# A hybrid decoder layer on one core: one copy moves to ScalarE, and large matrix products move between the stages of a recurrence

## The chip, the core and the metric

The kernel runs on one core of a Trainium2 chip. The core has five engines that work side by side: TensorE multiplies matrices (PE in the profile, with its weight loads as PEld), VectorE works on whole tiles (DVE), ScalarE copies and evaluates functions (ACT), GpSimd does some small work (POOL), and SyncE issues most of the transfers (SP). Each has its own list of instructions and goes through it in order; an instruction waits where its operands are not there yet. The metric is the device time of one execution in microseconds (us). Lower is better.

## The reference

The layer works on x, 512 positions of 2048 channels, in float32. Cut to what matters:

```python
h = rms_norm(x, norm_g)
z = h @ w_in          # r, k, v (1024 columns each), decay and rate inputs (64 each), gate (1024), pool input and pool gate (1024 each)
zs = zs + (token_shift(zs) - zs) * mu                      # r, k, v, decay and rate inputs
decay = exp(-exp(-softplus(-(w0 + tanh(wd) @ w_up)) - 0.5)); a = sigmoid(a0 + ad @ a_up)
kk = k * k_k;  kk = kk / max(norm of kk in each head, 1e-12);  k = k * (1 + (a - 1) * k_a)
# 16 heads of 64 channels; for each position t, with a state S of 64 x 64 in each head:
S = S (diag(w_t) - kk_t^T (a_t * kk_t)) + v_t^T k_t;   y_t = S r_t
y_rwkv = (head_group_norm(y) * ln_w + ln_b + bonus) * silu(gate)
d = trailing-window means of the pool input over 2, 4, 8, 16 positions, minus the input
y_pool = (d @ w_pool, per group of 256 channels) * pool_scale * silu(pool gate)
x = x + concat(y_rwkv, y_pool) @ w_out
x = x + sigmoid(x @ w_pg + b_pg) * (p @ w_ple)
out = rms_norm(x, final_g)
```

## The kernel before

*Large products.* Each large product is one matmul of 128 x 128 weights with 128 x 512 data. Float32 accuracy is reached by splitting both sides in two parts of a shorter format, `hi` and `lo` (`wsplit`, L132 and L133, for weights; `split`, L137 and L138, for data), and by three products per block (`mm3`, L156). The products of `h @ w_in` are made in blocks of 128 columns: `zk`, `zr`, `zv`, `zg` for the eight *pairs* of heads 0 to 7, and `zb` for sixteen *pool units*. A pool unit of the first kind ends in a chain of running sums on VectorE (L397 to L401, tiles `u` and `sw`); one of the second kind multiplies with `w_pool` (`pp`). All these products are one stream, `big`, 2,352 matmuls after the first normalisation. `pump(n)` issues the next n of them at the place where it stands in the code (in threes; `debt` carries what was too much). `need` issues as many as it takes until a given block is done. So the places and sizes of the pumps set what TensorE does while it would wait for the small work between them. The order on TensorE (PE) is the order of the code (`keep_in_program_order`). On VectorE and ScalarE the order is set by a scheduler that works with estimated times, so that an edit can change it at places far from the edit.

*The recurrence.* The 512 positions are cut into 8 chunks of 64, and within a chunk the recurrence is solved with an inverse of a triangular matrix. For each pair j these steps run:

- `prepare(j)` makes the operands `ar` and `bk` on VectorE (its last step is L541, the second half of `bk`), `scores(j)` multiplies them on TensorE (`pbo`, then `pm`) and sends the result through memory to the layout of the inversion, and `invert(j)` solves 32 x 32 triangles by 62 small VectorE steps (L593, L597).
- `gather(j)` completes the inverse. On TensorE: `pv` and `pbk` (transposes of v and `bk`, copied by ScalarE to `uv` and `bkn`), `pump(H4)`, `pmv` (the right-hand sides of all chunks in one psum tile, copied by ScalarE to `mv`, L648), `pss` (the norms of the *next* pair's keys; `norm_key`: ScalarE takes the root, L504, and VectorE the maximum, L505), `pump(H5)`, `pyt` (the transposes of the previous pair's result, `finish`: `yo` on ScalarE and VectorE, and its store to `yd`, L799), `pump(HX)`, then `pq` (from `y1`, a VectorE transpose at L669 that may only be issued behind L505) and `px`, each with `pump(H1)` behind it.
- `recur(j)` goes through the chunks. A chunk has three *hops*, each a small matmul whose result an engine copies for the next one: `py` (TensorE) to `zs` (VectorE, L721), `pu` to `uv` (ScalarE, L731), `ps` to the new state `sbd` (VectorE, L740 in the first chunk and L742 in the others; two tiles, `sbd0` and `sbd1`, take turns). A pump stands behind each hop: HC = (7, 7, 8) products. In the first chunk there is no state yet, so `zs` is a plain copy of `mv` (L725), and in place of the third pump `between` issues `pump(H3)`, the scores of the next pair and `pump(H2)`. Three steps of the next pair's inversion are made at each hop from the tenth on. After each fourth chunk, ScalarE copies `py` to `ysb` (L763), and after the last the group norm runs on VectorE (L772 to L787).

The sizes are H1 = 6, H2 = 16, H3 = 20, H4 = 6, H5 = 10, HX = 24.

*The end of the recurrence.* After pair 7, `pump(H2)` and `finish` of pair 7 are issued, then whatever is left in the stream (`pump(10 ** 6)`). ScalarE's queue loads `pn` (the embeddings p, L840) and the tiles `yin` (L858), which read back the sixteen stored blocks of `yd`. Both lie in memory that the recurrence's pool `rw` gives back when it closes, and wait until its last tile has been read, which is the store of pair 7's `yo`. TensorE transposes `pn` (`ppt`, split into `phi` and `plo`), and the products with `w_out` (`acc_o`) begin as soon as the first `yin` is split into `yhi` and `ylo`. Then come the products with `w_pg` (`acc_g`), the small `pple`, and the last normalisation.

Of the kernel before, what the change touches and what calls it, by code (L numbers as in the profile page):

```python
# [34 lines left out]
def trunk_kernel(ctx: ExitStack, tc: tile.TileContext, x, p, norm_g, w_in, mu, w0, w_up, a0, a_up,  # L35
                 k_k, k_a, r_k, ln_w, ln_b, w_pool, pool_scale, w_out, w_ple, w_pg, b_pg, final_g, out):
    nc = tc.nc
    PSUM = bass.MemoryType.PSUM
    x, p, w_in, w_out, w_ple, w_pg = x[0], p[0, 0], w_in[0], w_out[0], w_ple[0], w_pg[0]
# [303 lines left out]
    zsp = [rw.tile([P, P], F32, name=f"zs{i}") for i in range(2)]  # L343
# [93 lines left out]
    def pump(n):  # L437
        debt[0] += n
        while debt[0] > 0:
            c = next(big, None)  # L440
            if c is None:
                debt[0] = 0
                return
            debt[0] -= c
# [6 lines left out]

    pws, kks, late = {}, {}, [None]

    H1, H2, H3, H4, H5 = 6, 16, 20, 6, 10

    def decay_and_rate(j):

# [156 lines left out]
    def gather(j):  # L614
        d = st_[j]
        bk, v_, mt = d.pop("bk"), d.pop("v_"), d["mt"]
        if j + 1 < NJ:
            prepare_key(j + 1)
            decay_and_rate(j + 1)

        uv = rw.tile([P, NCH, P], F32, name=f"uv{j}", tag="uv")
        ps = psM.tile([P, T], F32, name=f"pv{j}", tag="m")
        for tt in range(NT):
            tr(ps[:, tt * P:(tt + 1) * P], v_[:, tt * P:(tt + 1) * P], ident)
        pv = ps.rearrange("p (t c) -> p t c", c=P)
        nc.scalar.copy(uv[0:64, 0::2, :], pv[0:64])
        nc.scalar.copy(uv[64:128, 1::2, :], pv[64:128])


        bkn = rw.tile([P, NCH, P], F32, name=f"bkn{j}", tag="bkn")  # L630
        for hf in range(2):
            ps = psM.tile([P, T], F32, name=f"pbk{j}_{hf}", tag="m")
            for i in range(4):
                ch = 4 * hf + i
                tr(ps[:, i * P:(i + 1) * P], bk[:, ch // 2, 2 * (ch % 2):2 * (ch % 2) + 2, :], ident)
            nc.scalar.copy(bkn[:, 4 * hf:4 * hf + 4, :], ps.rearrange("p (c n) -> p c n", n=P))

        pump(H4)

        ps = psM.tile([P, 8, C], F32, name=f"pmv{j}", tag="m")  # L640
        for u in range(8):
            for par in range(2):
                pb, kb = 64 * (1 - par), 64 * par
                h = u % 2
                mm(ps[pb:pb + 64, u, :], mt[kb:kb + 64, par, u, 1 - par, :],
                   uv[kb:kb + 64, 2 * (u // 2) + par, 64 * h:64 * h + 64], start=True, stop=True)
        mv = rw.tile([P, 4, P], F32, name=f"mv{j}", tag="mv")
        nc.scalar.copy(mv.rearrange("p q (h t) -> p (q h) t", h=2), ps)  # L648

        d.update(uv=uv, bkn=bkn, mv=mv)  # L650
        if j + 1 < NJ:
            norm_key(j + 1)
        pump(H5)
        if pending:
            pending.pop()()
        pump(HX)

        x1 = d["x1"]

        def units(fn):  # L660
            for u in range(8):
                for par in range(2):
                    fn(u, par, 64 * (1 - par))

        y1 = rw.tile([P, 8, 32], F32, name=f"y1{j}", tag="tm")

        with tc.issue_after(late[0].ins):
            for pb in (0, 64):
                yt = nc.vector.transpose(y1[pb:pb + 32], x1[pb:pb + 32, :, 0:32])  # L669
        if j + 1 < NJ:  # L670
            with tc.issue_after(yt.ins):
                scale_key(j + 1)
        ps3 = psM.tile([P, 8, 32], F32, name=f"pq2{j}", tag="m")
        units(lambda u, par, pb: mm(ps3[pb + 32:pb + 64, u, :],
                                                  mt[pb:pb + 32, par, u, 1 - par, 32:64],
                                                  y1[pb:pb + 32, u, :], start=True, stop=True,
                                                  tile_position=(pb, pb + 32)))
        q2t = rw.tile([P, 8, 32], F32, name=f"q2{j}", tag="xw")
        for pb in (0, 64):
            nc.scalar.copy(q2t[pb + 32:pb + 64], ps3[pb + 32:pb + 64])  # L680
        pump(H1)
        ps4 = psM.tile([P, 8, 32], F32, name=f"px2{j}", tag="m")
        units(lambda u, par, pb: mm(ps4[pb:pb + 32, u, :], q2t[pb + 32:pb + 64, u, :],
                                                  x1[pb + 32:pb + 64, u, 32:64], start=True, stop=True,
                                                  tile_position=(pb + 32, pb)))
        for pb in (0, 64):
            nc.scalar.copy(x1[pb:pb + 32, :, 32:64], ps4[pb:pb + 32])
        pump(H1)


    def recur(j, work, between):
        d = st_.pop(j)
        pw, ar, mt, bv, uv, bkn, mv, x1 = (d[n_] for n_ in ("pw", "ar", "mt", "bv", "uv", "bkn", "mv", "x1"))
# [15 lines left out]
        for ch in range(NCH):  # L709
            par, q = ch % 2, ch // 2  # L710
            pb = 64 * (1 - par)
            cur, nxt = sbd[ch % 2], sbd[(ch + 1) % 2]
            pcc = pw[:, ch, C:C + 1]
            sl = slice((ch % 4) * P, (ch % 4 + 1) * P)
            if ch % 4 == 0:
                py = psY.tile([P, T], F32, name=f"py{j}_{ch}", tag="y")
            zs = zsp[par]
            if ch > 0:
                mm(py[:, sl], ar[:, q, 2 * par:2 * par + 2, :], cur, start=ch in (1, 4), stop=True,
                                 skip_group_check=True)  # L720
                lead[0] = nc.vector.tensor_tensor(zs[pb:pb + 64], py[pb:pb + 64, sl], mv[pb:pb + 64, q, :], ALU.add)  # L721
                step()
                pump(HC1)
            else:
                nc.vector.tensor_copy(zs[pb:pb + 64], mv[pb:pb + 64, q, :])  # L725

            psu = psS.tile([P, T], F32, name=f"pu{j}_{ch}", tag="s")
            mm(psu[:, 0:P], x1[:, 2 * q:2 * q + 2, :], zs, start=True, stop=True)
            for h in range(2):
                hc = slice(64 * h, 64 * h + 64)  # L730
                nc.scalar.copy(uv[pb:pb + 64, ch, hc], psu[hc, hc])  # L731
            step()
            pump(HC2)
            if ch < NCH - 1:
                pss = psS.tile([P, T], F32, name=f"ps{j}_{ch}", tag="s")
                mm(pss[:, 0:P], bkn[:, ch, :], uv[:, ch, :], start=True, stop=True)
                for h in range(2):
                    hc = slice(64 * h, 64 * h + 64)
                    if ch == 0:
                        lead[0] = nc.vector.tensor_scalar(nxt[hc, hc], pss[hc, hc], pcc[hc], None, ALU.mult)  # L740
                    else:
                        lead[0] = nc.vector.scalar_tensor_tensor(nxt[hc, hc], pss[hc, hc], pcc[hc], s0p[hc, :],  # L742
                                                                 ALU.mult, ALU.add)
                s0p = rw.tile([P, C], F32, name=f"s0p{j}_{ch}", tag="s0p", bufs=2)
                pcn = pw[:, ch + 1, C:C + 1]
                if ch < NCH - 2:
                    for h in range(2):
                        hc = slice(64 * h, 64 * h + 64)
                        nc.gpsimd.tensor_scalar(s0p[hc, :], nxt[hc, hc], pcn[hc], None, ALU.mult)  # L749
            if ch % 4 == 3:  # L750
                for qq in range(2):
                    for h in range(2):
                        for pr in range(2):
                            c_ = ch - 3 + 2 * qq + pr
                            yr = slice(64 * pr, 64 * pr + 64)
                            o_ = (2 * qq + pr) * P + 64 * h
                            mm(py[yr, o_:o_ + 64], mt[:, pr, 2 * (c_ // 2) + h, pr, :],
                                             uv[:, c_, 64 * h:64 * h + 64], start=False, stop=True,
                                             skip_group_check=True)
                py4 = py.rearrange("p (s c) -> p s c", c=P)  # L760
                for pr in range(2):
                    yr = slice(64 * pr, 64 * pr + 64)
                    nc.scalar.copy(ysb[yr, q - 1:q + 1, :], py4[yr, pr::2, :])  # L763
            step()
            if ch == 0:
                between()
            else:
                pump(HC3)
# [31 lines left out]

        pending.append(finish)

    HC, HT, HX = (7, 7, 8), 130, 24
    HS, HN = 9, 3
    pending = []
    need("k", 0)
# [9 lines left out]
    for _ in invert(0):  # L816
        pass
    pump(HT)
    gather(0)
    for j in range(NJ):  # L820
        def between():
# [7 lines left out]
        recur(j, invert(j + 1) if j + 1 < NJ else iter(()), between)  # L829
        if j + 1 < NJ:  # L830
            gather(j + 1)
    pump(H2)
    pending.pop()()
    s2a.close()
    psB = ctx.enter_context(tc.tile_pool(name="psB", bufs=3, space=PSUM))
# [229 lines left out]
```

## Time and profile before

| | |
|---|---|
| median of 3 runs | 1123.04 us (1122.91 to 1123.46) |
| the profiled execution | 1124.35 us, its span 1122.6 us |
| mean granted TensorE clock | 0.993 of full speed |
| matmuls | 6,090 records, busy 96% of the span |
| VectorE, ScalarE, GpSimd | busy 63%, 41%, 7% |

How the rows that follow are read. The page's first part gives the busy time of each engine, its share of the span and its number of instructions. A row of a timeline has the start of an instruction in us, its duration, engine, line, operation and tiles, and in square brackets how long the engine had been idle and what ended that. A row of the chain of waits has the start and length of a step on the path that ended last. A row of TensorE's waits names the waiting tile, what released it, and then the sum in us, the number of waits and the longest. A row of a table by windows has the stretch, its length, then busy time and number of instructions of PE, PEld, DVE, ACT and POOL, the granted clock (1.00 is full speed), the busy share of the DMA engines and the rate in GB/s. A group's row gives its busy time and the mean duration in ns behind the bar. A matmul's recorded duration is longer than the distance to the next one, since they are pipelined.

### The profile page before, as it was taken

The page shows a single profiled execution, that of the slowest core. Times are in us where ns is not written, and L with a number is a line of the kernel's source. Part 1 is how long each engine was busy: PE and PEld are TensorE (multiplying, and loading weights), DVE is VectorE, ACT ScalarE, POOL GpSimd, SP SyncE. Part 2 cuts the span into 40 slices and gives each one's busy share as a digit, 9 for nine tenths or more (in the row PEclk, how much of TensorE's full clock was granted, in tenths as well). Part 3 has the DMA queues.
Part 4 walks back from the last instruction along what each step waited for, and adds up shares of the span by engine and source line. Part 5 has one row for each costly group of instructions (what it writes and reads, how often), then busy time and mean ns, then how long its engine had stood idle before and what let it go on. Part 6 is the DMA issues. An engine that isn't in the chain of part 4 may idle for free. (4 is left out here: it accounts for less than half of the span.)

```text
span 1122.6 us, 17272 instructions
## 1 busy us (share of the span) xinstructions
PE 1081.4 (96%) x6090; PEld 880.6 (78%) x6090; DVE 709.3 (63%) x1861; ACT 459.9 (41%) x920; POOL 75.2 (7%) x184
## 2 busy tenths in 40 slices
PE   5999999999999998999999999999999999999995
PEld 4888887877877876878778787778888888888885
DVE  6677868778588687687885955564243332525446
ACT  7643536336336353363362343252222232424333
POOL 2100010110110100101101102000000000000001
PEclk9999999999999998999999999999999999999998
DMA  7433332423423332324234233465343444434244
GB/s 228 122 92 96 101 105 69 114 85 82 121 78 93 99 77 71 100 74 110 79 89 120 74 104 96 150 215 174 115 161 125 138 145 155 150 104 151 94 132 150
DMA packets 173877, 130.17 MB, mean 116 GB/s; under 512 B 34165, under 2 KB 139230, under 8 KB 173790
## 3 DMA queue, kind: packets, MB, share of 16 engines
q1 hardware_dynamic: 157694, 103.89, 31.6%
q10 hardware_dynamic: 16096, 25.17, 6.9%
q8 instruction: 48, 0.79, 0.3%
q14 instruction: 39, 0.32, 0.1%
HBM read 113.82 MB, written 14.68 MB: 114 GB/s over the span
## 5 line engine op out<-in xcount | busy, mean ns | idle before, releaser
L133 DVE TENSOR_TENSOR wlo_g<-raw_g,whi_g 128x512 fp32r<-128x512 f32 x88 | 59.4, 684 | 78.6 <-ACT whi_g L132 78.4
L156 PE MATMUL zb<-hhi,whi_b 128*128 128x512 f32 x256 | 107.2, 419 | 0.0
L133 DVE TENSOR_TENSOR wlo_o<-raw_o,whi_o 128x512 fp32r<-128x512 f32 x64 | 43.8, 691 | 93.7 <-ACT whi_o L132 93.7
L156 PE MATMUL acc_o<-wlo_o,yhi 128*128 128x512 f32 x256 | 99.9, 390 | 0.6 <-DVE wlo_o L133 0.6
L156 PE MATMUL zb<-hhi,wlo_b 128*128 128x512 f32 x256 | 100.5, 392 | 0.0
L156 PE MATMUL acc_o<-whi_o,ylo 128*128 128x512 f32 x256 | 100.3, 392 | 0.0
L132 ACT CAST whi_g<-raw_g 128x512 fp32r<-128x512 f32 x88 | 54.3, 623 | 112.2 <-PE acc_g L156 62.1
L156 PE MATMUL zb<-hlo,whi_b 128*128 128x512 f32 x256 | 100.0, 391 | 0.0
L156 PE MATMUL acc_o<-whi_o,yhi 128*128 128x512 f32 x256 | 99.4, 391 | 0.5 <-ACT yhi L137 0.5
L156 PE MATMUL acc_g<-whi_g,x2hi 128*128 128x512 f32 x224 | 86.5, 386 | 0.0
L156 PE MATMUL acc_g<-wlo_g,x2hi 128*128 128x512 f32 x224 | 86.4, 386 | 0.0
L156 PE MATMUL acc_g<-whi_g,x2lo 128*128 128x512 f32 x224 | 86.3, 385 | 0.0
L132 ACT CAST whi_o<-raw_o 128x512 fp32r<-128x512 f32 x64 | 39.7, 623 | 101.1 <-PE acc_o L156 93.6
L749 POOL TENSOR_SCALAR s0p<-sbd,pw 64x64 f32<-64x64 f32 x96 | 52.9, 551 | 331.9 <-DVE sbd L742 255.3
L132 ACT CAST whi_b<-raw_b 128x512 fp32r<-128x512 f32 x64 | 39.6, 619 | 73.5 <-PE zv L156 27.7
L133 DVE TENSOR_TENSOR wlo_b<-raw_b,whi_b 128x512 fp32r<-128x512 f32 x64 | 43.8, 685 | 29.0 <-ACT whi_b L132 28.5
L156 PEld LDWEIGHTS acc_o<-wlo_o,yhi 128*128 128x128 f32 x256 | 48.1, 188 | 11.4 <-DVE wlo_o L133 1.5
L156 PEld LDWEIGHTS zb<-hhi,wlo_b 128*128 128x128 f32 x256 | 48.0, 188 | 10.9
L156 PEld LDWEIGHTS acc_o<-whi_o,yhi 128*128 128x128 f32 x256 | 48.1, 188 | 10.5 <-ACT yhi L137 0.7
L156 PEld LDWEIGHTS acc_o<-whi_o,ylo 128*128 128x128 f32 x256 | 48.1, 188 | 10.0 <-DVE ylo L138 0.4
L597 DVE TENSOR_TENSOR xw<-xw,tm 128x60 f32<-128x60 f32 (+24 forms) x248 | 51.9, 209 | 6.3
L156 PEld LDWEIGHTS zb<-hhi,whi_b 128*128 128x128 f32 x256 | 48.3, 189 | 8.7
(290 smaller groups left out, 2568.2 us busy)
## 6 DMA issues: line engine op xcount, KB each, us to landing
raw_b<-in_w_in_dram SPq DMA_DIRECT2D x64, 256.0 KB
raw_o<-in_w_out_dram SPq DMA_DIRECT2D x64, 256.0 KB
raw_g<-in_w_pg_dram SPq DMA_DIRECT2D x64, 256.0 KB
raw_k<-in_w_in_dram SPq DMA_DIRECT2D x32, 256.0 KB
raw_r<-in_w_in_dram SPq DMA_DIRECT2D x32, 256.0 KB
raw_v<-in_w_in_dram SPq DMA_DIRECT2D x32, 256.0 KB
raw_g<-in_w_in_dram SPq DMA_DIRECT2D x32, 256.0 KB
n<-nd SPq DMA_DIRECT2D x16, 256.0 KB
```

Source lines behind the costliest of these rows:

```text
L132: nc.scalar.copy(hi, raw)
L133: nc.vector.tensor_tensor(lo, raw, hi.bitcast(F32), ALU.subtract)
L156: i = nc.tensor.matmul(*a, **k)
L597: nc.vector.tensor_tensor(xw[:, 0:n_, s + 1:32], xw[:, 0:n_, s + 1:32], tm[:, 0:n_, 0:w_], ALU.add)
L749: nc.gpsimd.tensor_scalar(s0p[hc, :], nxt[hc, hc], pcn[hc], None, ALU.mult)
```

## The change

Three things are edited. The copy of the first chunk's right-hand side to `zs` no longer stands in `recur` as a VectorE copy from `mv` (L725 before); ScalarE makes it in `gather`, straight from the psum tile of `pmv`, ahead of the `mv` copy. Large products are placed otherwise: H3 from 20 to 16, H4 from 6 to 8, HC from (7, 7, 8) to (8, 8, 8), HX from 24 to 16. And the pump ahead of pair 7's `finish` takes 32 products (HE) instead of 16 (H2). The stream itself is the same.

```diff
-    H1, H2, H3, H4, H5 = 6, 16, 20, 6, 10
+    H1, H2, H3, H4, H5, HE = 6, 16, 16, 8, 10, 32
...
         mv = rw.tile([P, 4, P], F32, name=f"mv{j}", tag="mv")
+        nc.scalar.copy(zsp[0][64:128, :].rearrange("p (h t) -> p h t", h=2), ps[64:128, 0:2, :])
         nc.scalar.copy(mv.rearrange("p q (h t) -> p (q h) t", h=2), ps)
...
                 step()
                 pump(HC1)
-            else:
-                nc.vector.tensor_copy(zs[pb:pb + 64], mv[pb:pb + 64, q, :])
...
-    HC, HT, HX = (7, 7, 8), 130, 24
+    HC, HT, HX = (8, 8, 8), 130, 16
...
         if j + 1 < NJ:
             gather(j + 1)
-    pump(H2)
+    pump(HE)
     pending.pop()()
```

In the changed kernel the new copy is L648, lines 649 to 723 stand one further down, and lines from 724 on one further up.

VectorE of the kernel before, at the beginning of pair 4's recurrence: the end of `prepare(5)` (L540, L541), a pool unit's running sums (`sw4`, `u4`) and the copy to `zs0`.

```order
L397 TENSOR_TENSOR sw4_1_5273<-u4_5271 128x511
L398 COPY sw4_1_5273<-u4_5271 128x1
L540 TENSOR_TENSOR kk5_5098<-kk5_5098,tha5_5125 128x512
L397 TENSOR_TENSOR sw4_2_5276<-sw4_1_5273 128x510
L398 COPY sw4_2_5276<-sw4_1_5273 128x2
L541 TENSOR_TENSOR bk5_5301<-kk5_5098,ipw5_5118 128x4x128
L400 TENSOR_TENSOR sw4_2_5276<-sw4_2_5276,rc1_504 128x4
L725 COPY zs0_566<-mv4_5171 64x128
L401 SCALAR_TENSOR_TENSOR u4_5271<-sw4_2_5276,u4_5271 128x512
```

The copy stands behind L541 and most of the running sums. In the changed kernel it stands on ScalarE, in pair 4's gather:

```order
L636 COPY bkn4_5150<-pbk4_1_5157 128x512
L462 CAST uaz0_568<-ur6_5302 64x128
L461 CAST as6_5309<-ar6_5306 128x128
L462 CAST uaz1_569<-ar6_5306 64x128
L648 COPY zs0_566<-pmv4_5172 64x128
L649 COPY mv4_5189<-pmv4_5172 128x512
L504 ACT_TABLE_LOAD
L504 ACTIVATE kk5_5113<-pss5_5192 128x512
```

It is now directly ahead of `mv`, and the root of the next pair's norms (L504) comes behind both.

VectorE in pair 5's gather, from the maximum of pair 6's norms (L505) to their reciprocal (L509), before:

```order
L505 TENSOR_SCALAR kk6_5803<-kk6_5803 128x512
L669 STREAM_TRANSPOSE y15_5939<-x15_5706 32x256
L133 TENSOR_TENSOR wlo_g6_1_3263<-raw_g6_1_3260,whi_g6_1_3262 128x512
L797 TENSOR_TENSOR yo4_5897<-yo4_5897,bv4_4613 128x512
L669 STREAM_TRANSPOSE y15_5939<-x15_5706 32x256
L798 TENSOR_TENSOR yo4_5897<-yo4_5897,sg4_4703 128x512
L133 TENSOR_TENSOR wlo_g6_2_3269<-raw_g6_2_3266,whi_g6_2_3268 128x512
L509 RECIPROCAL kk6_5803<-kk6_5803 128x512
```

and in the changed kernel:

```order
L505 TENSOR_SCALAR kk6_5824<-kk6_5824 128x512
L133 TENSOR_TENSOR wlo_g6_3_3291<-raw_g6_3_3288,whi_g6_3_3290 128x512
L397 TENSOR_TENSOR sw5_1_5916<-u5_5914 128x511
L398 COPY sw5_1_5916<-u5_5914 128x1
L796 TENSOR_TENSOR yo4_5935<-yo4_5935,bv4_4628 128x512
L397 TENSOR_TENSOR sw5_2_5919<-sw5_1_5916 128x510
L398 COPY sw5_2_5919<-sw5_1_5916 128x2
L797 TENSOR_TENSOR yo4_5935<-yo4_5935,sg4_4699 128x512
L133 TENSOR_TENSOR wlo_k7_0_3297<-raw_k7_0_3294,whi_k7_0_3296 128x512
L400 TENSOR_TENSOR sw5_2_5919<-sw5_2_5919,rc1_504 128x4
L670 STREAM_TRANSPOSE y15_5955<-x15_5724 32x256
L401 SCALAR_TENSOR_TENSOR u5_5914<-sw5_2_5919,u5_5914 128x512
```

Between L505 and the two transposes of `y1` stand a pool unit's sums, two weight parts and both steps of `yo`, where one weight part and one step of `yo` stood.

TensorE around the transposes of pair 7's result (`pyt7`), the last step of the recurrence, before:

```order
L156 MATMUL zb15_7774<-hhi_134,wlo_b15_0_4676 128x512
L160 MATMUL pyt7_7784<-ident_94,ysb7_7374 128x128 x4
L156 MATMUL zb15_7774<-hhi_134,whi_b15_0_4675 128x512
L156 MATMUL zb15_7774<-hlo_135,whi_b15_0_4675 128x512
L156 MATMUL zb15_7774<-hhi_134,wlo_b15_0_4676 128x512
L156 MATMUL zb15_7774<-hhi_134,whi_b15_1_4681 128x512
```

and after:

```order
L156 MATMUL pp15_7826<-dl3_7518,whi_wp15_0_4740 128x512
L156 MATMUL pp15_7826<-dh3_7517,wlo_wp15_0_4741 128x512
L160 MATMUL pyt7_7835<-ident_94,ysb7_7399 128x128 x4
L848 MATMUL ppt0_7860<-ident_94,pn0_7854 128x128 x2
L848 MATMUL ppt1_7867<-ident_94,pn0_7854 128x128
L848 MATMUL ppt0_7860<-ident_94,pn1_7856 128x128 x2
L848 MATMUL ppt1_7867<-ident_94,pn0_7854 128x128
L848 MATMUL ppt1_7867<-ident_94,pn1_7856 128x128 x2
L156 MATMUL acc_o0_0_7946<-whi_o0_8_7952,yhi_7877 128x512
```

`pyt7` had 24 large products between pair 7's last `py` and itself, and 45 behind it before `ppt`; now 33 stand ahead of it and none behind it.

## Prediction

> **What bounds the kernel now.** I read the page's busy shares first, then TensorE's waits, then the timelines at the longest waits, and last the chain that ended last.
>
> ```profile
> PE 1081.4 (96%) x6090; PEld 880.6 (78%) x6090; DVE 709.3 (63%) x1861; ACT 459.9 (41%) x920; POOL 75.2 (7%) x184
> ...
> 871.19 41.06 PE acc_o L156 x181
> ...
> PE py L156 <- DVE sbd L742: 4.2, 7, 1.5
> PE pu L156 <- issue: 3.3, 1, 3.3
> ...
> PE pu L156 <- DVE zs L721: 2.6, 5, 0.6
> PE ps L156 <- ACT uv L731: 2.3, 3, 1.2
> PE pyt L160 <- DVE ysb L787: 1.6, 3, 1.1
> PE pss L156 <- ACT bkn L636: 1.4, 2, 0.8
> ...
> 154.20:179.30 25.10, 23.89 (x127) 19.15 (x126) 21.40 (x90) 9.85 (x22) 3.15 (x7) 1.00 0.29 82
> ...
> 613.70:640.20 26.50, 24.45 (x129) 19.62 (x129) 23.55 (x98) 8.11 (x20) 3.26 (x6) 1.00 0.26 75
> sum 177.60, PE 170.42 PEld 135.39 DVE 153.33 ACT 65.14 POOL 22.80; mean PE 24.35 PEld 19.34 DVE 21.90 ACT 9.31 POOL 3.26
> ```
>
> TensorE is the bound: 96%. A large product costs 41.06/181 = 0.227 us, although its row shows 0.39, so each wait in the list hides another 0.16. The three hop rows (py, pu behind zs, ps) are 4.2 + 2.6 + 2.3 = 9.1 us in 15 waits; with 15 x 0.16, and 7 x 0.16 for py's second matmul, which then comes 0.21 instead of 0.05 after the first, that is 12.6. Waits too short for the list add some 1.6 by the same spacing (my estimate): 14.2. They lie where VectorE also inverts the next pair: the windows are these stretches of pairs 0 to 6 (first, last, sum of seven), VectorE busy 86% and TensorE idle 7.2 us. So the time is TensorE's work, which the change leaves alone, plus its waits.
>
> **The change, part by part.**
>
> (1) *The copy of the first right-hand side.* In pair 4 VectorE reaches it late:
>
> ```profile
> 431.49 0.39 PE L156 MATMUL zg<-hhi,wlo_g 128*128 128x512 f32 x1
> 435.19 0.76 PE L156 MATMUL pu<-zs,x 128*128 128x128 f32 x2 [3.31 <-issue]
> ...
> 434.08 0.68 DVE L541 TENSOR_TENSOR bk<-kk,ipw 128x512 f32<-128x512 f32 x1
> ...
> 434.87 0.22 DVE L725 COPY zs<-mv 64x128 f32<-64x128 f32 x1
> ...
> 434.38:441.21 6.83, 6.02 (x16) 4.98 (x17) 3.23 (x8) 1.65 (x4) 1.26 (x2) 0.50 0.02 6
> ```
>
> `pu` starts 435.19 - 431.49 - 0.23 = 3.5 us late, right behind L725, which stands after `prepare`'s chain; the list calls it "issue". The granted clock then is 0.50 until 441.21: half of 6.02 us, 3.0 more. On ScalarE the copy stands directly behind `pmv`, long before this hop: **-6.5**. In the other seven pairs L725 comes early and covers nothing. VectorE loses 8 x 0.22 us, off the path. ScalarE's copy has no row; the nearest lie on both sides:
>
> ```profile
> L731 ACT COPY uv<-pu 64x64 f32<-64x64 f32 x128 | 26.5, 207 | 57.2 <-PE pu L156 55.9
> L763 ACT COPY ysb<-py 64x256 f32<-64x256 f32 x32 | 11.7, 367 | 16.8 <-PE py L156 16.1 <-DVE wlo_wp L133 0.5
> ```
>
> 0.21 to 0.37; by size I take 0.25. Behind it wait the `mv` copy, the table load and the square root, hence L505 and y1: counted in (4).
>
> (2) *More products in the hops* (7, 7, 8 become 8, 8, 8). A chunk has 24 products instead of 22 on average, 0.45 us more.
>
> ```profile
> 624.69 0.38 PE L156 MATMUL py<-sbd,ar 128*128 128x128 f32 x2
> 631.97 0.49 PE L156 MATMUL py<-sbd,ar 128*128 128x128 f32 x2 [1.50 <-DVE sbd L742]
> 638.31 0.49 PE L156 MATMUL py<-sbd,ar 128*128 128x128 f32 x2 [0.55 <-DVE sbd L742]
> ```
>
> Here a chunk took 7.3 and 6.3 us because sbd came late; without waits it takes about 5.7. Over an inversion stretch some four chunks bring 4 x 0.45 = 1.8 us of cover, against waits of 14.2/8 = 1.8 per pair. Bounds: none of it lands on a wait (0) and all does (-14.2). The waits bunch in the last chunks, and in pair 6, where the pool unit's chain stands between two hops, most must stay. I take **-10.0**, nearer the upper end since cover and need are equal.
>
> (3) *`pyt`, `pss`.* `pmv` often has 9 products ahead of it instead of 6, +0.7 us for the copies: of 1.4 (pss) and about 1.3 (pyt in pair 4) I take half: **-1.4** (0 to -2.7).
>
> (4) *Fewer products in the gather stage* (24 to 16 ahead of `pq`). From `pss` to `pq` 6 to 9 products go, up to 9 x 0.227 = 2.0 us. `pq` needs y1, which VectorE makes after L505:
>
> ```profile
> 190.65 0.50 PE L156 MATMUL pss<-kqh,blk 128*128 128x512 f32 x1
> 199.30 0.69 PE L156 MATMUL pq<-y,mt 32*32 32x32 f32 x32
> ...
> 197.22 0.44 DVE L669 STREAM_TRANSPOSE y<-x 32x256 f32<-32x256 f32 x1
> ...
> 499.51 0.50 PE L156 MATMUL pss<-kqh,blk 128*128 128x512 f32 x1
> 508.16 0.69 PE L156 MATMUL pq<-y,mt 32*32 32x32 f32 x32
> ...
> 503.45 0.42 DVE L505 TENSOR_SCALAR kk<-kk 128x512 f32<-128x512 f32 x1
> 505.42 0.44 DVE L669 STREAM_TRANSPOSE y<-x 32x256 f32<-32x256 f32 x1
> ...
> L397 DVE TENSOR_TENSOR sw<-u 128x511 f32<-128x511 f32 x8 | 5.5, 690 | 0.0
> ```
>
> Gather 1: pss to pq shrinks from 8.65 to 6.6; y1 ended 7.0 after pss, and the new order puts two more 128x512 operations before its second half (2 x 0.65), less 0.6 because the bkn copies no longer hold ScalarE: 7.7. Wait 1.1. Gather 5: pss to pq is 7.3; y1 now stands behind the pool unit's two long sums, two `wlo` and two `yo` steps: about 5.3 us after L505, itself 4.0 after pss, so 9.3. Wait 2.0. Elsewhere 0 to 0.2. Sum **+3.3** (0 if VectorE runs ahead of L505, 5 if it is behind). Next late is L541 ahead of `pm` in pair 5: its order has about one long operation more and `pm` 3 to 6 products less: **+0.9** (0 to 1.5). At the other `pm` L541 keeps more room.
>
> So before the recurrence's end TensorE saves S = 6.5 + 10.0 + 1.4 - 3.3 - 0.9 = 13.7.
>
> (5) *The end of the recurrence.* When pair 7's last `py` issues, 36 more large products have been done than before (counted in the order): 36 x 0.227 = **+8.2** earlier work. That is no gain by itself, since what follows is a chain of latency:
>
> ```profile
> 709.50 0.66 PE py L156 x16
> ...
> 716.31 1.89 DVE ysb L787 x8
> ...
> 718.24 0.33 PE pyt L160
> 718.57 2.49 PE zb L156 x11
> 721.08 3.33 DMA yd<-yo
> ...
> 724.52 0.39 ACTq L840
> ...
> 725.47 4.48 DMA yin<-yd
> 729.98 0.62 ACT yhi L137
> ...
> 730.65 0.50 PE L156 MATMUL acc_o<-whi_o,yhi 128*128 128x512 f32 x1 [0.48 <-ACT yhi L137]
> ...
> PE acc_o L156 <- DVE wlo_o L133: 0.6, 2, 0.4
> ```
>
> The `pn` and `yin` loads stand on ScalarE's queue behind the store of pair 7's `yo` and wait for it to land, then 4.5 us for the load: `acc_o` comes 730.65 - 709.50 = 21.2 us after `py`. Before, 69 products cover this; the new order has 33 ahead of `pyt` and none behind it. The chain itself keeps its length: `ysb` needs about 7.9 us from `py`, the 33 products and `py` itself 8.1. So `acc_o` still comes 21.2 after `py`, and TensorE stands idle for some 11 us between `pyt` and the `pn` landing. Pumping 32 instead of 16 at the end hides the wait of `pyt` and lengthens this gap; nothing is won. Raw weight loads on SyncE only follow the buffers; POOL's work is untouched.
>
> In (1) a wait of 3.5 us cost the clock 3.0 us; I take **+3.0** here too (0 to 3.4, half of 6.83). [...] Then +0.6 because `phi` and `plo` now stand ahead of the first `yhi` and `ylo`, and -1.0 because the first weight splits are made during the gap (0.6 listed plus hidden spacing).
>
> Sum: -13.7 + 8.2 + 3.0 + 0.6 - 1.0 = -2.9. The profiled execution takes 1124.35 us at a span of 1122.6; the runs' median is 1123.04, and I take the difference from that: **1120.1 us**. About 0.2% (2.2 us) is what a measurement of this kernel can tell from no change.
>
> **The rivals.** The end costs 8.2 + 3.0 + 0.6 - 1.0 = 10.8; everything turns on S.
>
> *Nothing measurable.* S between 8.6 and 13.0: the hops fill by 8 instead of 10, about 1122. For it: VectorE is 86% busy in the hops, and what moves out of the gather stage comes back as waits on y1. Against it: pair 4 is sure.
>
> *Slower.* The end's gap takes what the moved products covered, and S stays under 8.6. Place: between `pyt` and `acc_o`; price 10.8; it decides if the hops give back under 5. With 4, S = 7.7 and the time is 1126. For it: the chain's rows above are already tight (TensorE waits 0.48 for `yhi` today). Against it: equal cover and need in (2).
>
> *The copy does not help.* ScalarE's copy comes as late as L725 did: pair 4 keeps 6.5, time 1126.6. Against it: it stands between `pmv` and `mv`, and seven pairs show `mv` done in time.
>
> *Much faster.* The `yin` loads run ahead of pair 7's store and the gap does not open: S and the old `pyt` wait count in full, about 1108. Against it: the chain waits for the store, and the new order keeps that.
>
> **How the numbers follow.** Forecast 0.50 (its own range 1116 to 1120.8), nothing measurable 0.28, slower through the end 0.13, copy useless 0.05, much faster 0.04. So faster 0.54, same 0.28, slower 0.18. The range 1114.5 to 1125.5 is S from 8.3 to 19.3: the upper bound of (2) with no wait in (4), and the hops giving 5; outside lie some 2 in 10.
>
> **What would show it.** Changed profile: no wait of `pu` at pair 4 and no clock dip there; hop waits near 3 us in sum; waits of `pq` on y1 in gathers 1 and 5; an idle TensorE of about 11 us between the last `pyt` and `ppt`, with the clock at half behind it. I am wrong if the end's gap is much shorter than 8 us, if the hop waits stay above 7, or if `pq` or `pm` wait above 8 in all.

## The result: slower by half a per cent

The changed kernel takes 1129.49 us (four runs, 1127.87 to 1130.2) where the kernel before took 1123.25 us; the ratio is 1.0053, 95% interval 1.0035 to 1.007. The forecast was 1120.1 us.

The profiled execution of the changed kernel is the fastest of its four runs (1127.87 us, span 1126.2), and that of before was slower than its median (1124.35 against 1123.04). So the two traces differ by 3.6 us, and the medians by 6.2; a second profile of the changed kernel (after_again, below) is 1.2 us longer than the first. What follows is read from the traces.

The busy shares of the changed kernel and its list of TensorE's waits, without those of the first 59 us (behind the colon the sum in us, the number and the longest):

```profile
PE 1079.2 (96%) x6090; PEld 882.3 (78%) x6090; DVE 708.1 (63%) x1853; ACT 463.3 (41%) x928; POOL 72.4 (6%) x184
...
PE ppt L848 <- DMA pn<-in_p_dram: 8.9, 1, 8.9
...
PE py L156 <- DVE sbd L741: 5.1, 7, 1.1
...
PE pq L156 <- DVE y L670: 3.1, 2, 1.8
PE pss L156 <- ACT bkn L636: 1.2, 2, 0.8
PE pp L156 <- ACT uv L627: 0.9, 1, 0.9
PE pu L156 <- ACT x L688: 0.9, 1, 0.9
PE pmv L156 <- ACT bkn L636: 0.9, 1, 0.9
...
PE pu L156 <- DVE zs L722: 0.8, 1, 0.8
...
PE pm L156 <- DVE bk L541: 0.3, 1, 0.3
PE ps L156 <- ACT uv L730: 0.3, 1, 0.3
```

The 3.3 us of `pu` ("issue") have gone, and the waits of `ps` and of `pu` behind `zs` are nearly gone. But `py` waits longer than before (5.1 for 4.2), `pq` waits 3.1 where it did not wait, and one new wait is larger than all of these: 8.9 us of `ppt` for the load of p.

That wait is the end of the recurrence. The chain that ended last, from pair 7's last `py` to the first product with `w_out`, and TensorE's busy time and granted clock (the figure behind POOL's) in the same stretch:

```profile
713.00 0.61 PE py L156 x16
713.62 6.37 PE zb L156 x27
719.99 1.38 PE pp L156 x6
...
724.52 2.96 DMA yd<-yo
...
727.57 0.39 ACTq L839
...
728.53 4.08 DMA yin<-yd
732.61 0.02 issue
732.63 0.62 ACT yhi L137
733.25 0.04 issue
733.30 31.71 PE acc_o L156 x128
...
713.00:721.20 8.20, 8.20 (x51) 6.74 (x51) 6.35 (x32) 3.24 (x7) 0.00 (x0) 1.00 0.26 84
721.20:730.60 9.40, 0.59 (x5) 0.35 (x3) 3.25 (x6) 1.35 (x2) 0.00 (x0) 0.69 0.53 171
730.60:733.30 2.70, 1.94 (x9) 1.53 (x9) 0.69 (x2) 1.26 (x3) 0.00 (x0) 0.50 0.78 270
733.30:738.00 4.70, 4.70 (x11) 3.69 (x12) 2.47 (x4) 1.47 (x3) 0.00 (x0) 0.50 0.48 156
```

After `pyt` TensorE is idle for 9 us; the clock falls to 0.50 and stays there into `acc_o`, where 11 products take 4.7 us.

Three times say where the 3.6 us are (the last `py` is taken at the first of its 16 matmuls). Last `py`: 709.43 before, 712.93 after (+3.5, although 36 products or 8.2 us of work more are done by then, so 4.7 were saved). First `acc_o`: 730.65 and 733.30, that is 21.2 and 20.4 behind `py` (-0.8). End: 1122.6 and 1126.2, that is 392.0 and 392.9 behind `acc_o` (+0.9).

For the experiments one more measure is used: the distance from the product ahead of a small matmul to that matmul, less the usual distance of such a pair (0.23 us for a hop's matmul), summed from 59 us to the last `py`. It holds the waits that the list leaves out or shows without the hidden 0.16 us. "Hops" is the sum over `py`, `pu` and `ps` (the expectations below give hc_back's as 9.2, against a slightly other usual distance). In the column `pq`, 2.3 us are no wait: the kernel before has them too, and none of its eight `pq` comes late; they lie between the 32 matmuls of each `pq`. hc_back's profiled execution is the slowest of its five (1116.58 us):

| kernel | HC | hops | pq | pyt | last py | first acc_o |
|---|---|---|---|---|---|---|
| before | 7, 7, 8 | 19.4 (16.0 without pair 4's `pu`) | 2.3 | 1.3 | 709.43 | 730.65 |
| changed | 8, 8, 8 | 11.8 | 5.5 | 0.7 | 712.93 | 733.30 |
| copy_only | 7, 7, 8 | 15.3 | 2.3 | 1.3 | 703.99 | 725.00 |
| hc_back | 7, 7, 8 | 9.5 | 2.3 | 5.1 | 682.68 | 721.07 |
| ht142 | 7, 7, 8 | 12.8 | 3.2 | 3.2 | 688.40 | 722.42 |
| ht154 | 7, 7, 8 | 11.9 | 4.6 | 2.3 | 690.51 | 721.79 |
| best2 | 7, 7, 8 | 13.8 | 2.3 | 0.2 | 692.48 | 719.05 |
| after_defer | 8, 8, 8 | 9.0 | 5.5 | 0.7 | 710.61 | 731.02 |
| hcb_defer | 7, 7, 8 | 10.2 | 2.3 | 5.1 | 682.44 | 720.84 |
| best3 | 7, 7, 8 | 9.8 | 2.3 | 0.2 | 688.02 | 714.58 |

### The profile page after: what moved, and what is told of

It reads as the page before. It is cut to its first block, busy times and chain, and to the rows that moved or that the text cites. A ratio compares the mean times of both kernels' runs of the same rounds, so it can differ in the third digit from the quotient of the medians.

```text
span 1126.2 us, 17257 instructions
## 1 busy us (share of the span) xinstructions
PE 1079.2 (96%) x6090; PEld 882.3 (78%) x6090; DVE 708.1 (63%) x1853; ACT 463.3 (41%) x928; POOL 72.4 (6%) x184
## 4 chain that ended last, share of the span: by engine, by line
PE 47%; DVE 4%; ACT 1%; issue 1%; DMA 1%; ACTq 0%; DVEq 0%
PE acc_o L156 16%; PE acc_g L156 14%; PE zb L156 9%; PE zg L156 2%; PE zk L156 1%; PE py L156 1%; PE zr L156 1%; PE px L942 1%; PE pple L919 1%; PE pple L920 1%; PE pple L918 1%; PE pp L156 1%; PE pu L156 0%; DVE tm L593 0%; DMA yin<-yd 0%
## 5 line engine op out<-in xcount | busy, mean ns | idle before, releaser
L133 DVE TENSOR_TENSOR wlo_g<-raw_g,whi_g 128x512 fp32r<-128x512 f32 x88 | 59.7, 685 | 79.5 <-ACT whi_g L132 79.4
L133 DVE TENSOR_TENSOR wlo_o<-raw_o,whi_o 128x512 fp32r<-128x512 f32 x64 | 43.9, 690 | 94.8 <-ACT whi_o L132 94.8
L132 ACT CAST whi_g<-raw_g 128x512 fp32r<-128x512 f32 x88 | 54.3, 622 | 103.7 <-PE acc_g L156 65.9
L132 ACT CAST whi_o<-raw_o 128x512 fp32r<-128x512 f32 x64 | 39.9, 623 | 105.2 <-PE acc_o L156 97.2
L748 POOL TENSOR_SCALAR s0p<-sbd,pw 64x64 f32<-64x64 f32 x96 | 49.9, 520 | 340.9 <-DVE sbd L741 260.2
L132 ACT CAST whi_b<-raw_b 128x512 fp32r<-128x512 f32 x64 | 39.7, 620 | 75.0 <-PE zv L156 32.5
L133 DVE TENSOR_TENSOR wlo_b<-raw_b,whi_b 128x512 fp32r<-128x512 f32 x64 | 43.9, 686 | 36.0 <-ACT whi_b L132 33.4
L156 PEld LDWEIGHTS acc_o<-whi_o,ylo 128*128 128x128 f32 x256 | 48.6, 190 | 10.2 <-DVE ylo L138 0.2
```

The costliest lines, as they stand in the source:

```text
L132: nc.scalar.copy(hi, raw)
L133: nc.vector.tensor_tensor(lo, raw, hi.bitcast(F32), ALU.subtract)
L156: i = nc.tensor.matmul(*a, **k)
```

## The experiments

### The parts of the change alone

copy_only is the kernel before with `+ nc.scalar.copy(zsp[0][64:128, :]...)` in `gather` and without the VectorE copy in `recur`.

> The kernel before with the ScalarE copy alone; all pump sizes are those of before. Theory A (the changed kernel's slowdown comes from the end, the copy is good): pair 4's wait of pu (3.5 us) and the clock dip behind it (3.0 us) go, the products behind the recurrence stay at 24 and 45, so 1123.25 - 6.5 = 1116.7 us. Theory B (the copy only moves the wait: ScalarE makes mv, the root and y1 later, and VectorE's new order puts another long operation before a hop): 1122 to 1125 us, with new waits of pq or py that sum to 4 us or more.

Measured: 1118.29 us against 1122.32, ratio 0.9958 (0.9946 to 0.9971). Pair 4's wait and the clock dip are gone (hops 19.4 to 15.3, last `py` 5.4 us earlier, the mean granted clock 0.996 where the profile of before has 0.993), and no wait took their place: theory A, at 4 us of the 6.5 by the medians and 6.0 by the spans (the profiled execution of before was 1.3 us above its median).

pumps_only is the changed kernel with the copy back on VectorE:

```diff
-        nc.scalar.copy(zsp[0][64:128, :].rearrange("p (h t) -> p h t", h=2), ps[64:128, 0:2, :])
...
                 pump(HC1)
+            else:
+                nc.vector.tensor_copy(zs[pb:pb + 64], mv[pb:pb + 64, q, :])
```

> The changed kernel with the first right-hand side copied by VectorE again (as before); the pump sizes are the new ones. Theory A: the copy is late again in pair 4, behind prepare's chain; 1129.5 + 6.5 = 1136 us, and pu waits some 3.5 us there. Theory B (the new sizes alone change VectorE's order so that the copy comes in time): 1129.5 us, no such wait.

Measured: 1136.84 us, ratio 1.0122 (1.0108 to 1.0136), about 7 us above the changed kernel, as theory A says, but at other places: the new sizes do change VectorE's order, pair 4 is in time, and pairs 2 and 6 are late.

```profile
PE pu L156 <- issue: 5.1, 2, 3.0
...
283.33 0.46 PE L156 MATMUL pu<-zs,x 128*128 128x128 f32 x2 [2.11 <-issue]
...
282.29 0.68 DVE L539 SCALAR_TENSOR_TENSOR ar<-kk,pw 128x512 f32<-128x512 f32 x1
283.01 0.22 DVE L725 COPY zs<-mv 64x128 f32<-64x128 f32 x1
```

So the copy on ScalarE is worth 4 us with the old sizes and 7 with the new ones, and the new sizes alone cost more than the change as a whole.

### The end of the recurrence

gap_filled puts work that is not used into the gap:

```diff
     pump(HE)
     pending.pop()()
+    pump(10 ** 6)
+    fill = psA.tile([P, T], F32, name="fill", tag="acc")
+    for i in range(40):
+        mm(fill, hhi[:, 0, 0:P], hhi[:, i % KT, :], start=True, stop=True)
```

> The changed kernel with 40 added products of 128x128 by 128x512 between pair 7's last transposes and the transposes of p (their result is not used): 40 x 0.227 = 9.1 us more work for TensorE. Theory A (TensorE stands idle there, waiting for the store of pair 7's yo and the loads behind it, and the idle time halves the clock for the first products behind it): the work costs nothing, the clock stays at 1.00, and acc_o runs 2 to 3 us shorter: 1127 us. Theory B (the 11 us are no idle time that work could fill, or the clock has another cause): 1136 to 1139 us.

Measured: 1125.69 us, ratio 1.0028 (1.0017 to 1.004), 3 to 4 us faster than the changed kernel with 9.4 us more work on TensorE. The windows and the timeline:

```profile
721.50:731.00 9.50, 9.50 (x45) 7.72 (x45) 2.77 (x5) 0.88 (x2) 0.00 (x0) 1.00 0.58 187
731.00:738.00 7.00, 5.78 (x28) 4.69 (x28) 4.04 (x7) 3.83 (x8) 0.00 (x0) 1.00 0.57 188
...
721.36 9.37 PE L156 MATMUL fill<-hhi 128*128 128x512 f32 x40
730.56 1.14 PE L852 MATMUL ppt<-ident,pn 128*128 128x128 f32 x8
732.92 0.50 PE L156 MATMUL acc_o<-whi_o,yhi 128*128 128x512 f32 x1 [1.22 <-ACT yhi L137]
```

`ppt` starts at 730.56, where it started at 730.65 without the filling: the gap is nothing but idle time. With the clock at 1.00 the stretch from the first `acc_o` to the end is 390.5 us instead of 392.9: the half clock cost 2.4 us.

yo7_pp takes away what the loads wait for:

```diff
-            yo = rw.tile([P, T], F32, name=f"yo{j}", tag="t", bufs=4)
+            yo = pp.tile([P, T], F32, name=f"yo{j}", tag="u") if j == NJ - 1 else \
+                rw.tile([P, T], F32, name=f"yo{j}", tag="t", bufs=4)
```

> The changed kernel with pair 7's yo in a tile of another pool, so that the loads of p and yin need not wait until the store of yo has read it. Theory A (that store's 3.0 us lie on the chain from the last py to acc_o, and nothing covers it): the loads start 3 us earlier, 1129.5 - 3.0 = 1126.5 us. Theory B (the loads wait for something else of the recurrence's pool or for their queue, or the DMA takes as long whenever it starts): 1129.5 us.

Measured: 1126.71 us, ratio 1.0035 (1.0023 to 1.0048). The chain no longer holds the store:

```profile
725.65 0.33 ACTq L799
...
726.08 0.44 ACTq L840
...
727.65 4.24 DMA yin<-yd
731.89 0.57 ACT phi L137
732.46 0.53 ACT yhi L137
732.99 0.04 issue
733.03 2.08 PE acc_o L156 x4
```

The loads of p follow the issue of the store by 0.4 us where they followed by 3.05. But `acc_o` comes 19.0 us behind `py` instead of 20.4: of 3.0 us freed, 1.4 arrive. `ppt`, which needs p, now starts 4.5 us after the issue of the load (726.08 to 730.54) instead of 3.1. The store and other transfers run at the same time; that they are what slows the load is not shown. Theory A in kind. Its size is 1.4 us by this chain and 2.4 to 2.8 by the medians (1129.11 and 1129.49 to 1126.71); the profiled execution is the slowest of its six.

copy_he32 is copy_only with `pump(32)` ahead of pair 7's `finish`.

> The ScalarE copy and the pump of 32 ahead of pair 7's finish, all other sizes of before: 39 products ahead of pyt instead of 24, 30 behind it instead of 45. Theory A (from the last py on the chain over pyt, the store and the loads sets the time, so products ahead of pyt delay it once pyt no longer waits): pyt comes 1.6 us later than with the copy alone and everything behind it too, 1.6 us above copy_only. Theory B (TensorE's work sets the time, and the wait of pyt that goes is won): 2.5 us below copy_only.

Measured: 1119.09 us, ratio 0.9965 (0.9952 to 0.9977), beside copy_only's 0.9958. `pyt` no longer waits and comes 9.6 us behind `py` instead of 7.5, and `acc_o` 21.6 instead of 21.0. Theory B's gain of 2.5 us is not there: removing this wait of TensorE is worth nothing, since the chain sets the time. Theory A's 1.6 us was too much. The profile of copy_he32 also has a stretch of half clock that copy_only's does not have (724.49 to 727.91); the mean granted clock of its five executions is 0.993 to 0.996, that of copy_only's 0.995 to 0.997.

hc_back is the changed kernel with one number back:

```diff
-    HC, HT, HX = (8, 8, 8), 130, 16
+    HC, HT, HX = (7, 7, 8), 130, 16
```

> The changed kernel with HC back at (7, 7, 8): 120 products fewer in the hops, which then stand behind pair 7's last py (39 ahead of pyt, 114 behind it), so the end's chain is covered. With X for what the hops' extra products saved in waits, the last py comes at 713.0 - 27.2 + X and acc_o 153 x 0.227 + 3.1 us after it. Theory A (X is about 4, as the spacing in the two traces says): acc_o at 727.6, no half clock, about 4 us below the kernel before. Theory B (X is 10, as forecast, and the changed kernel lost it elsewhere): about 2 us above the kernel before.

Measured: 1113.28 us against 1123.18, ratio 0.9917 (0.9903 to 0.9932): 16 us below the changed kernel and 10 below before, further than theory A. There is no gap (`acc_o` 38.4 us behind `py` for 153 products and the small work), the waits of `pq` are gone, and the hops, with 120 products fewer, wait less: 9.5 us instead of 11.8. The extra products in the hops show no saving. A saving of some 3 us cannot be excluded, since the hops' sum moves by as much with the position of the blocks alone (next section); one of 10, as forecast, can.

### What sets the hops' waits

ht142 and ht154 are hc_back with HT 142 and 154, nothing else.

> hc_back with HT 142 instead of 130: 12 more products during pair 0's inversion, hence the whole stream a quarter of a block further on in every later hop; the number of products in each hop is the same, and 102 still stand behind pyt. Theory P (a hop waits where the end of a block of 48 products falls on it, since the block's long operations on VectorE and ScalarE, the shift or the square, then stand ahead of the hop's copy; so the position of the blocks sets the waits): the waits of py, pu and ps lie at other places, and their sum differs from hc_back's 9.2 us (by start-to-start spacing over the normal one) by 2 us or more. Theory C (a hop's waits are set by how many products cover it): the same waits at the same places, sum within 1 us, time as hc_back's 1113.

> hc_back with HT 154: half a block further on (24 products); 90 products behind pyt. Theory P: again other places and a sum that differs from hc_back's and from ht142's by 2 us or more. Theory C: as hc_back.

Measured: 1116.69 us, ratio 0.9944 (0.993 to 0.9957), and 1116.16 us, ratio 0.9939 (0.9926 to 0.9951). Hop waits of 12.8 and 11.9 us against hc_back's 9.5, and `pq` at 3.2 and 4.6 against 2.3, with the same numbers of products in every hop and in every gather stage (the two profiles of the changed kernel agree within 0.1 us in this sum). The two differ from each other by only 0.9, less than theory P asked; theory C, which wants the same sum in all three, is out.

In the changed kernel, one such wait: VectorE's rows ahead of the state `sbd`, and TensorE's row that waits for it.

```profile
177.65 0.75 DVE L353 SCALAR_TENSOR_TENSOR sr<-zr,prm,sr 128x511 f32<-128x511 f32 x1
178.32 0.17 DVE L597 TENSOR_TENSOR xw<-xw,tm 128x16 f32<-128x16 f32 x1
178.40 0.59 DVE L741 SCALAR_TENSOR_TENSOR sbd<-ps,pw,s0p 64x64 f32<-64x64 f32 x2
...
179.05 0.49 PE L156 MATMUL py<-sbd,ar 128*128 128x128 f32 x2 [0.89 <-DVE sbd L741]
```

The block `zr` ended in this hop, and its shift (L353) stands ahead of `sbd`. Three kernels put only that behind the copy: the block's last two operations (`end`, the calls of `silu2` or `shifted` as before) wait in a list, which `recur` works off behind `zs` and behind `sbd` (`lead`; `uvc` is the last copy to `uv`), ahead of the pump there:

```diff
+    def flush(*behind):
+        with ExitStack() as es:
+            for i in behind:
+                if i is not None:
+                    es.enter_context(tc.issue_after(i.ins))
+            while ends:
+                ends.pop(0)()
...
+            ends.append(end)
+            if not hold[0]:
+                flush()
...
                 step()
+                flush(lead[0], uvc)
                 pump(HC1)
...
             step()
+            flush(lead[0], uvc)
```

> The changed kernel once more, beside the next three. Its four times of before lie between 1127.9 and 1130.2, wider than its rivals'. Theory A: the stretch of half clock behind the end's gap differs from run to run, and this profile shows another length of it: 1128 to 1130 us. Theory B (the spread has another cause): the stretch is as in the first profile, 11 us from 726 to 737.

> The changed kernel with one thing added: where a block of r, k, v or the gate ends within a hop, its two operations (the scaling on ScalarE, the shift on VectorE, or the gate's tanh and product) are written behind the hop's copy and queued behind it on their engine. TensorE's order and all pump sizes are the same. Theory P (hop waits come from long operations at a block's end ahead of the hop's copy): the four waits with the shift right ahead (1.06, 0.92, 1.26 and 0.23 us) go, the sum of the hops' waits falls from 11.8 to about 8.3, 3.5 us below the changed kernel. Theory C (VectorE is simply full there, the operation only delays the next hop instead): the sum stays within 1 us, same time.

Measured side by side: 1129.11 us for the changed kernel (ratio 1.0061, 1.0047 to 1.0075), 1125.75 us with the deferral (ratio 1.0031, 1.002 to 1.0043). The hops' sum falls from 11.8 to 9.0, `py` comes 2.3 us earlier than in the first profile of the changed kernel and 3.6 earlier than in the second. The same hop:

```profile
176.50 0.28 DVE L760 SCALAR_TENSOR_TENSOR sbd<-ps,pw,s0p 64x64 f32<-64x64 f32 x1
...
177.41 0.75 DVE L353 SCALAR_TENSOR_TENSOR sr<-zr,prm,sr 128x511 f32<-128x511 f32 x1
...
177.23 0.49 PE L156 MATMUL py<-sbd,ar 128*128 128x128 f32 x2 [0.25 <-DVE sbd L760]
```

The shift now starts behind `sbd`, and 0.25 us of 0.89 are left. That is theory P. after_again also tells where two executions of the changed kernel differ. The half clock at the end is as long in both (13.7 us; 392.9 us from `acc_o` to the end), so its theory A is out. But in pair 5's gather, where `pq` waits 1.84 us in both, the granted clock behind the wait is 1.00 in the first profile and 0.50 from 507.40 to 510.81 in the second. There the last `py` comes 1.2 us later (714.17 for 712.93), and the span is 1.2 us longer (1127.4 for 1126.2, at a mean granted clock of 0.988 for 0.990).

best2 is hc_back with `H4 = 11`, `H5 = 13`, `HE = 36`; hcb_defer and best3 are hc_back and best2 with the deferral.

> hc_back with H4 11 and H5 13 (3 more products each ahead of pss and pyt, which wait there for bkn and ysb, 1.5 and 3.0 us in sum) and HE 36; 63 products stay behind pyt, enough for the chain. Theory A (products are free as long as the end's chain stays covered, so put them where a wait is): these waits go, 2 to 4 us below hc_back, about 1110. Theory P says besides that the blocks' positions move, which can give or take 3 us.

> hc_back with the same deferral. Theory P: the waits with the shift ahead (0.97, 0.80, 1.26 us) go: 3 us below hc_back, about 1110 us. Theory C: 1113 us.

> best2 with the same deferral. Theory P: the waits with the shift or the gate's operation ahead (0.19, 1.71, 0.37, 0.37, 0.82, 0.74 us) go, 3 to 4 us below best2, about 1110 us. Theory C: 1114 us.

Measured: best2 1113.74 us, ratio 0.9919 (0.9907 to 0.9932), no gain over hc_back: the waits of `pss` and `pyt` went as asked (`pyt` 5.1 to 0.2), and the hops took as much (9.5 to 13.8). hcb_defer 1114.0 us, ratio 0.9928 (0.9916 to 0.9941), no gain either: the three waits behind a shift shrank, and others came, behind weight splits (L132, L133) and the square of the keys, so the sum stays near 10; here theory C describes it. best3 1109.83 us, ratio 0.9889 (0.9876 to 0.9903): the hops fall from 13.8 to 9.8 us and the time by 3.9, theory P. Its waits:

```profile
PE py L156 <- DVE sbd L760: 4.5, 8, 1.2
...
PE acc_o L156 <- ACT whi_o L132: 2.1, 2, 1.3
PE pm L156 <- DVE sgp L417: 0.8, 1, 0.8
```

best3 is the fastest kernel of this study, 12 us below before. What the deferral gives depends on how many hops had a block's end in them, and some 9 to 10 us of hop waits stayed in each kernel that has it.

### Two more versions

y1_free takes away the rule that `y1` is issued behind the maximum (`with tc.issue_after(late[0].ins):`).

> The changed kernel without the rule that y1's transposes are issued behind the maximum of the next pair's norms. Theory A (pq waits in gathers 1 and 5 because of what the order puts between that maximum and y1): y1 comes early, both waits (3.1 us) go, the last py and all behind it come 3 us earlier: 1129.5 - 3 = 1126.5 us. Theory B (x1 itself comes late there, or VectorE is simply full, so that the wait goes elsewhere): 1129 to 1131 us.

Measured: 1132.96 us, ratio 1.0089 (1.0073 to 1.0104), 3.5 us above the changed kernel. `pq`'s sum falls from 5.5 to 2.3 as theory A says, but in pair 0 `y1` now stands at the head of VectorE's queue and waits for its load, with the operations behind it that ScalarE waits for ahead of `bkn`, and `pss` behind that:

```profile
115.69 0.43 DVE L669 STREAM_TRANSPOSE y<-x 32x256 f32<-32x256 f32 x1 [4.13 <-DMA x<-xd]
...
PE pss L156 <- ACT bkn L636: 5.2, 3, 4.1
```

best1 is copy_only with a shorter chain at the end: p is loaded into tiles of the recurrence that pair 7 has no use for, `ppt` stands directly behind `pyt`, `phi` and `plo` are made only behind the tenth `yin`, and pair 7's `yo` is in `pp` as in yo7_pp:

```diff
+    H1, H2, H3, H4, H5 = 6, 16, 16, 6, 10
...
+    HC, HT, HX = (7, 8, 8), 118, 24
...
+        t_ = rw.tile([P, 2, DPLE], F32, name=f"pn{h}", tag=("tha", "ipw")[h])
...
+    pump(32)
     pending.pop()()
+    ppt = []
+    for k in range(2):
+        pt = psM.tile([P, T], F32, name=f"ppt{k}", tag="m")
```

> The ScalarE copy; p loaded into the recurrence's own memory during pair 7 and transposed right behind pyt; pair 7's yo in another pool; HC (7, 8, 8), H3 16, HT 118 and 32 products ahead of pair 7's finish, which moves 15 products ahead of the last py. Theory A (the chain from the last py to acc_o is what the moved products run into; without the store and the two loads of p it is 3 to 4 us shorter, so that 15 products can be moved for nothing; HC2 is the size that removes the waits of ps, 3.5 us): 3 us below copy_only. Theory B (the chain stays as long): 1 to 3 us above copy_only.

Measured: 1115.05 us, ratio 0.9928 (0.9916 to 0.9941), 3.2 us below copy_only, theory A. `acc_o` comes 16.3 us behind `py` instead of 21.0, and the 15 products moved ahead of `py` cost it 1.7 us instead of 3.4: the hops wait less (10.7 for 15.3), `pss` waits more (3.2 for 1.5).

## Where the prediction was right and where it failed

The outcome is the rival called "slower", at 0.13: the end's gap takes what the moved products covered, decided by whether the hops give back under 5. They gave back 4.1 (16.0 to 11.8, rounded), and S, the saving before the recurrence's end, is 4.7 instead of 13.7 (3.4 in the second profile). Of the 9.0 us that S lacks, 5.9 are in step (2).

- (1), the copy, -6.5: right in its mechanism; of the size, the 3.5 us of the wait are shown, and the 3.0 for the clock were read from one execution. copy_only measured 4.0 by the medians and 6.0 by the spans, pumps_only about 7 the other way, but at pairs 2 and 6. In the changed kernel's trace the wait is 3.5 as said, and the large products' own spacing, which held the half clock, fell by 1.6 instead of 3.0.
- (2), more products in the hops, -10.0: the step that failed. The sum went from 16.0 to 11.8, and hc_back, at 9.5 with 120 products fewer in the hops, gives no sign that even this is owed to the products. The step took 14.2 us of waits as time that any product nearby would cover ("cover and need are equal"). It put the second matmul of `py` 0.05 us behind the first where nothing waits; in the trace of before the distance is 0.11 in 45 pairs and 0.21 in the other 11, which makes that term 0.7 us instead of 1.1. Most are waits behind single long operations, of 0.6 us on ScalarE and 0.7 us on VectorE, at the places where a block or a pool unit ends or a weight split falls; other pump sizes move those places, and the sum goes anywhere between 9.5 and 16.0 us at one HC, (7, 7, 8). The rows shown for it had this in them: the wait of 1.50 us at 631.97 is longer than what one more product, 0.23 us, covers.
- (3), -1.4: `pyt` gained 0.6, while `pmv` lost 0.9 and a pool unit's `pp` waits 0.9 for a psum tile that `uv` still reads: together, with smaller ones, 0.8 lost.
- (4), +3.3 and +0.9: 3.2 for `pq`, at the two gathers named and near the waits named (listed as 1.23 and 1.84; 1.1 and 2.0 were said), and 0.6 for `pm`. The cause was half right: hc_back has the same HX, and no new wait of `pq`. The order on VectorE makes it, and that order hangs on where the blocks lie: HT alone brings 0.9 and 2.3 us of it back in ht142 and ht154. Not in the sum is the half clock behind one such wait in the second profile (507.40 to 510.81), where the last `py` comes 1.2 us later than in the first.
- (5), +10.8 for the end: 8.3. The idle time is 8.9 us (11 were said), the half clock 2.4 (3.0), the chain from `py` 0.8 shorter. That the 16 more products ahead of `pyt` win nothing, as was said, is shown by copy_he32.

From the parts, S = 3.5 + 1.6 + 4.1 - 0.8 - 3.2 - 0.6 = 4.6, against 4.7 from the last `py`. The 8.3 are the 8.2 us of moved work, less 0.8 for the chain, plus 0.9 behind `acc_o`; so -4.7 + 8.3 = +3.6, the difference of the two traces. The two misses, 9.0 in S and 2.5 at the end, partly cancel.

The stated range does not come out of the terms named for it: (2) at its upper bound with no wait in (4) gives S = 21.2, and hops that give 5 give S = 8.7, where 19.3 and 8.3 were written.

## What to carry to other kernels

Work that fills a bottleneck engine's waits is a fixed stock: each product spent earlier is missing at the last latency chain, so count what covers that chain (here about 70 products for 21 us) before moving anything ahead of it, and shorten the chain first. Before buying cover for a list of waits, look at what stands right ahead of each late producer on its own engine: a wait behind one long operation can go when that operation is queued behind the producer (2.8 and 4.0 us of hop waits in two kernels, nothing in a third), where 120 products more in the hops brought no saving. And where a scheduler orders the other engines, any change of a pump size moves the whole pattern, so sizes have to be tried, not summed.

## What the runs showed of the hardware that was not expected

In these traces the clock does not follow the length of a wait alone. In pumps_only a wait of 2.11 us (up to 283.33) was followed by half clock, beginning after work had resumed, and a wait of 2.97 us (up to 596.58) by none:

```profile
282.00:283.30 1.30, 0.00 (x0) 0.00 (x0) 1.24 (x4) 1.29 (x2) 0.00 (x0) 1.00 0.55 201
283.30:284.50 1.20, 1.17 (x5) 1.03 (x6) 1.17 (x2) 0.68 (x3) 0.00 (x0) 0.83 0.64 182
284.50:285.50 1.00, 1.00 (x4) 0.81 (x3) 0.78 (x2) 0.00 (x0) 0.00 (x0) 0.50 0.16 46
285.50:286.50 1.00, 1.00 (x4) 0.81 (x3) 0.47 (x1) 0.62 (x1) 0.00 (x0) 0.50 0.00 0
286.50:287.50 1.00, 1.00 (x5) 0.81 (x5) 0.88 (x2) 0.00 (x0) 0.00 (x0) 0.50 0.00 0
287.50:288.50 1.00, 1.00 (x6) 0.82 (x6) 0.56 (x2) 0.00 (x0) 0.43 (x1) 1.00 0.76 263
...
593.00:596.50 3.50, 0.62 (x3) 0.19 (x1) 3.45 (x7) 1.08 (x2) 0.00 (x0) 1.00 0.47 137
596.50:598.00 1.50, 1.42 (x7) 1.27 (x8) 0.69 (x1) 0.41 (x2) 0.00 (x0) 1.00 0.10 30
598.00:600.00 2.00, 2.00 (x11) 1.67 (x10) 0.74 (x3) 0.80 (x2) 0.86 (x2) 1.00 0.00 0
```

The shorter wait was followed by some 3.4 us of half clock (an estimate: the 0.83 of the second row puts the fall at 284.1 us, and the clock is back at 1.00 from 287.50 on). The same difference stands between two executions of one kernel: in pair 5's gather of the changed kernel `pq` waits 1.84 us in both profiles, and the granted clock behind that wait is 1.00 in the first (506.80 to 512.00) and 0.50 from 507.40 to 510.81 in the second. So a wait of about 2 us was followed by half clock in some places and not in others. What tells them apart is not shown: no run here was made to vary it. The longest stretch of half clock in the changed kernel's profile is the one at the end of its recurrence, 13.7 us (724.8 to 738.5), where TensorE was idle for 8.9 us (up to 730.65).
